# RMSNorm with tanh-GELU on one core: six rows per partition instead of four, in units of three, with one last store and one gamma transfer

## The chip, the cores and the metric

One core of one Trainium2 chip. The time is the device time of one execution in microseconds (us). "Before" and "after" name the two kernels. A statement such as "317.44 us" is a median of single executions; a ratio is the mean time of one kernel's fast runs over the mean of the other kernel's fast runs of the same rounds, so it is not quite the ratio of the medians quoted beside it. An interval is 95%. A run is called slow when it is over 1.5% above the fastest of the same kernel.

## The reference

```python
# x: 8 x 1024 x 2048 float32, gamma: 2048, eps = 1e-5
rms = np.sqrt(np.mean(x ** 2, axis=-1, keepdims=True) + eps)
out = gamma * x / rms
return 0.5 * out * (1 + np.tanh(np.sqrt(2 / np.pi) * (out + 0.044715 * out ** 3)))
```

There are 8192 rows of 8 KB: 67.1 MB in, 67.1 MB out, and little arithmetic per byte.

## The kernel before

A group is 128 partitions times four rows. Row r of partition p lies beside row r+1 of the same partition in HBM, so one partition's share of a group is one contiguous piece of 32 KB. Six buffers on chip hold six groups. ACT (ScalarE) squares and sums each row, GpSimd makes 1/rms from the sum, VectorE multiplies by gamma (which TensorE has spread over the partitions into PSUM), ACT applies the GELU with 1/rms as its scale, and the store goes out from ACT's queue. Loads go out from SyncE's queue.

```python
ROWS = 4
SLOTS = 6
...
store_pieces = {
    0: [(R, [(0, NARROW), (NARROW, R * D)])],            # a narrow first store of 512 B per partition
    G - 1: [(1, [(r * D, r * D + D)]) for r in range(R)], # last group: a store per row
}
...
def load(g):
    nc.sync.dma_start(out=slot[g % SLOTS], in_=x3[g])
...
for g in range(G + 1):
    if g < G:
        squares(g)
        inverse_rms(g)
        scale(g)
    if g:
        gelu_store(g - 1)                  # one group behind
        if g - 1 + SLOTS < G:
            load(g - 1 + SLOTS)            # waits for that store to land
```

Of the kernel before, what the change touches and what calls it, by code (L numbers as in the profile page):

```python
# [1 line left out]

# [4 lines left out]

FP32 = mybir.dt.float32
ALU = mybir.AluOpType
ACT = mybir.ActivationFunctionType  # L10

P = 128
ROWS = 4
SLOTS = 6

GW = 32
CHUNK = 512

NARROW = 128


@with_exitstack
def kernel(
    ctx: ExitStack,
    tc: tile.TileContext,
    x: bass.AP,
    gamma: bass.AP,
    eps: bass.AP,
    out: bass.AP,
):  # L30




    nc = tc.nc
    D = x.shape[-1]
    R = ROWS
    eps_f = float(eps)
    x3 = x.rearrange("b s d -> (b s) d").rearrange("(g p r) d -> g p r d", p=P, r=R)
    o3 = out.rearrange("b s d -> (b s) d").rearrange("(g p r) d -> g p r d", p=P, r=R)  # L40
    G = x3.shape[0]

    sbuf = ctx.enter_context(tc.tile_pool(name="sbuf", bufs=1))
    psum = ctx.enter_context(
        tc.tile_pool(name="psum", bufs=1, space=bass.MemoryType.PSUM)
    )
    slot = [sbuf.tile([P, R, D], FP32, name=f"slot{i}") for i in range(SLOTS)]
    gamma_row = sbuf.tile([1, D // GW, GW + 4], FP32, name="gamma_row")
    ones = sbuf.tile([1, P], FP32, name="ones")
    warm = sbuf.tile([1, 1], FP32, name="warm")  # L50
    power = sbuf.tile([P, R], FP32, name="power")
    ssq = sbuf.tile([P, G, R], FP32, name="ssq")
    rstd = sbuf.tile([P, G, R], FP32, name="rstd")
    ms = sbuf.tile([P, R], FP32, name="ms")
    y = sbuf.tile([P, R], FP32, name="y")
    z = sbuf.tile([P, R], FP32, name="z")
    gamma_ps = psum.tile([P, D], FP32, name="gamma_ps")
    junk = psum.tile([P, D], FP32, name="junk")


    whole = [(R, [(0, R * D)])]
    store_pieces = {
        0: [(R, [(0, NARROW), (NARROW, R * D)])],
        G - 1: [(1, [(r * D, r * D + D)]) for r in range(R)],
    }
    scale_pieces = {G - 1: [(0, 1), (1, 1), (2, 1), (3, 1)]}

    def load(g):
        nc.sync.dma_start(out=slot[g % SLOTS], in_=x3[g])  # L69

    def squares(g):
        for r in range(R):
            nc.scalar.activation(  # L73
                out=junk,
                in_=slot[g % SLOTS][:, r, :],
                func=ACT.Square,
                accum_out=ssq[:, g, r : r + 1],
            )

    def scale(g):  # L80
        for r, n in scale_pieces.get(g, [(0, R)]):
            rows = slot[g % SLOTS][:, r : r + n, :]
            nc.vector.tensor_tensor(  # L83
                out=rows,
                in0=rows,
                in1=gamma_ps.unsqueeze(1).to_broadcast([P, n, D]),
                op=ALU.mult,
            )

    def inverse_rms(g):  # L90

        v = nc.gpsimd
        v.tensor_scalar(  # L93
            out=ms, in0=ssq[:, g, :], scalar1=1.0 / D, scalar2=eps_f,
            op0=ALU.mult, op1=ALU.add,
        )
        v.tensor_tensor(out=y, in0=ms, in1=power, op=ALU.pow)  # L97
        v.tensor_tensor(out=z, in0=y, in1=y, op=ALU.mult)  # L98
        v.tensor_tensor(out=z, in0=z, in1=ms, op=ALU.mult)  # L99
        v.tensor_scalar(  # L100
            out=z, in0=z, scalar1=-0.5, scalar2=1.5, op0=ALU.mult, op1=ALU.add
        )
        v.tensor_tensor(out=rstd[:, g, :], in0=z, in1=y, op=ALU.mult)  # L103

    def gelu_store(g):
        flat = slot[g % SLOTS].rearrange("p r d -> p (r d)")
        dst = o3[g].rearrange("p r d -> p (r d)")
        row = 0
        for n, stores in store_pieces.get(g, whole):
            for r in range(row, row + n):  # L110
                nc.scalar.activation(  # L111
                    out=slot[g % SLOTS][:, r, :],
                    in_=slot[g % SLOTS][:, r, :],
                    func=ACT.Gelu_apprx_tanh,
                    scale=rstd[:, g, r : r + 1],
                )
            row += n
            for a, b in stores:
                nc.scalar.dma_start(out=dst[:, a:b], in_=flat[:, a:b])  # L119

    with tc.manual_schedule():
        for k in range(0, D, CHUNK):
            nc.scalar.dma_start(
                out=gamma_row[:, k // GW : (k + CHUNK) // GW, 0:GW],
                in_=gamma[k : k + CHUNK].rearrange("(o a b) -> o a b", o=1, b=GW),
            )
        for g in range(SLOTS):
            load(g)
        nc.gpsimd.memset(power, -0.5)  # L129
        nc.vector.memset(warm, 0.0)  # L130
        nc.vector.memset(ones, 1.0)  # L131
        nc.scalar.activation(out=warm, in_=warm, func=ACT.Gelu_apprx_tanh)  # L132
        for k in range(0, D, CHUNK):
            nc.tensor.matmul(  # L134
                out=gamma_ps[:, k : k + CHUNK],
                lhsT=ones,
                rhs=gamma_row[:, k // GW : (k + CHUNK) // GW, 0:GW],
                start=True,
                stop=True,
            )  # L140
        for g in range(G + 1):
            if g < G:
                squares(g)
                inverse_rms(g)
                scale(g)
            if g:
                gelu_store(g - 1)
                if g - 1 + SLOTS < G:
                    load(g - 1 + SLOTS)


# [1 line left out]
_INS = ['x', 'gamma', 'eps']  # L153
_OUTS = [((8, 1024, 2048), 'float32')]

_NUMBERS = {'eps': 9.999999747378752e-06}


# [26 lines left out]
```

## Time and profile before

| | before |
|---|---|
| time, median of the first 3 runs | 317.41 us (317.26 to 317.46) |
| span of the profiled run | 315.5 us |
| ACT / VectorE busy | 80% / 44% |
| DMA queues, share of the 16 engines' span | 49.7% + 49.4% |
| HBM traffic | 425 GB/s over the span |

The page is read from the share of busy time to the slices to the DMA queues. The prediction shows the lines and reads them.

One thing goes beyond the page. The trace holds a record of each DMA packet (queue, start, duration, bytes). No view prints it; where a number below comes from it, I say "packet record".

### The profile page before, as it was taken

The numbers are of one execution on the slowest core, as the hardware profiler recorded it, in microseconds if no ns is written. First come the engines' busy times: TensorE is split into PE (matmuls) and PEld (weight loads), VectorE is DVE, ScalarE is ACT, GpSimd is POOL, SyncE is SP. The second block draws the span as 40 slices with busy tenths as digits, with TensorE's granted clock in tenths as the row PEclk, the third lists the DMA queues.
The fourth block names the chain that finished last, engine by engine and source line by source line (L and its number), as shares of the span: only waits on it lengthen the run. The fifth ranks groups of instructions, "written<-read, shape, count | busy, mean of one in ns | idle before, by whom it ended". The sixth has DMA issues, their size and how long they took to land.

```text
span 315.5 us, 479 instructions
## 1 busy us (share of the span) xinstructions
PE 7.9 (3%) x8; PEld 2.1 (1%) x8; DVE 139.4 (44%) x21; ACT 251.2 (80%) x194; POOL 32.3 (10%) x101
## 2 busy tenths in 40 slices
PE   0810000000000000000000000000000000000000
PEld 0200000000000000000000000000000000000000
DVE  0028909091918282827328082370824609480000
ACT  1289999999999999989596895969959599598500
POOL 0020202020202020202020020200202002020000
DMA  8999999999999999999999999999999999999997
GB/s 329 404 461 403 459 413 396 453 406 462 403 461 407 457 407 458 411 453 416 449 428 440 432 432 432 432 440 424 446 416 453 411 453 411 453 415 449 416 418 314
DMA packets 5315, 134.25 MB, mean 426 GB/s; under 512 B 704, under 2 KB 832, under 8 KB 832
## 3 DMA queue, kind: packets, MB, share of 16 engines
q1 hardware_dynamic: 2304, 67.11, 49.7%
q10 hardware_dynamic: 3008, 67.12, 49.4%
q14 instruction: 3, 0.02, 0.0%
HBM read 67.12 MB, written 67.11 MB: 425 GB/s over the span
## 4 chain that ended last, share of the span: by engine, by line
ACT 38%; DMA 32%; another core or an unknown queue 18%; issue 5%; ACTq 1%; SPq 0%
ACT slot L111 21%; DMA slot<-in_x_dram 16%; ACT junk L73 16%; DMA out_dram<-slot 15%; ACTq L119 1%; SPq L69 0%; ACTq L111 0%; ACTq L73 0%
## 5 line engine op out<-in xcount | busy, mean ns | idle before, releaser
L83 DVE TENSOR_TENSOR slot<-slot,gamma_ps 128x8192 f32<-128x8192 f32 (+1 forms) x19 | 139.2, 7338 | 142.3 <-ACT junk L73 142.3
L73 ACT ACTIVATE junk<-slot 128x2048 f32<-128x2048 f32 x64 | 120.4, 1881 | 40.8 <-DMA slot<-in_x_dram 36.8
L111 ACT ACTIVATE slot<-slot,rstd 128x2048 f32<-128x2048 f32 x64 | 123.0, 1987 | 1.7 <-ACT slot L111 1.7
L93 POOL TENSOR_SCALAR ms<-ssq 128x4 f32<-128x4 f32 x16 | 3.1, 194 | 242.8 <-ACT junk L73 242.8
L97 POOL TENSOR_TENSOR y<-ms,power 128x4 f32<-128x4 f32 x16 | 16.1, 1009 | 1.3
L73 ACT ACTIVATION_READ_ACCUMULATOR junk<-slot 128x1 f32 x64 | 11.9, 186 | 0.0
L134 PE MATMUL gamma_ps<-gamma_row,ones 1*128 1x512 f32 x8 | 7.9, 1112 | 9.2 <-DMA gamma_row<-in_gamma_dram 9.2
L132 ACT ACT_TABLE_LOAD x1 | 1.3, 1283 | 3.3 <-issue 3.3
L99 POOL TENSOR_TENSOR z<-z,ms 128x4 f32<-128x4 f32 x16 | 3.2, 201 | 1.3
L103 POOL TENSOR_TENSOR rstd<-z,y 128x4 f32<-128x4 f32 x16 | 3.2, 200 | 1.3
L98 POOL TENSOR_TENSOR z<-y 128x4 f32<-128x4 f32 x16 | 3.2, 200 | 1.3
L100 POOL TENSOR_SCALAR z<-z 128x4 f32<-128x4 f32 x16 | 3.1, 195 | 1.4
L134 PEld LDWEIGHTS gamma_ps<-gamma_row,ones 1*128 1x128 f32 x8 | 2.1, 306 | 13.4 <-issue 8.7
L130 DVE MEMSET warm<- 1x1 f32 x1 | 0.1, 59 | 0.8 <-PEq L166 0.8
L132 ACT ACTIVATE warm<-warm 1x1 f32<-1x1 f32 x1 | 0.2, 203 | 0.0
L131 DVE MEMSET ones<- 1x128 f32 x1 | 0.2, 165 | 0.0
L129 POOL MEMSET power<- 128x4 f32 x1 | 0.1, 102 | 0.3 <-POOLq L166 0.3
L166 POOL MEMSET const-float32-0.0<- 128x1 f32 x1 | 0.1, 99 | 0.2 <-issue 0.2
L166 POOL MEMSET const-bfloat16-1.0<- 128x1 bf16 x1 | 0.1, 102 | 0.0
L166 POOL MEMSET const-uint8-127<- 128x1 uint8 x1 | 0.1, 102 | 0.0
L166 POOL MEMSET const-float32-1.0<- 128x1 f32 x1 | 0.1, 99 | 0.0
## 6 DMA issues: line engine op xcount, KB each, us to landing
slot<-in_x_dram SPq DMA_DIRECT2D x16, 4096.0 KB, 29.9
out_dram<-slot ACTq DMA_DIRECT2D x14, 4096.0 KB, 43.3
out_dram<-slot ACTq DMA_DIRECT2D x4, 1024.0 KB, 17.5
out_dram<-slot ACTq DMA_DIRECT2D x1, 4032.0 KB, 28.5
gamma_row<-in_gamma_dram ACTq DMA_DIRECT2D x4, 2.0 KB, 10.3
out_dram<-slot ACTq DMA_DIRECT2D x1, 64.0 KB, 14.4
```

The lines of the kernel that those rows point to most:

```text
L73: nc.scalar.activation(out=junk, in_=slot[g % SLOTS][:, r, :], func=ACT.Square, accum_out=ssq[:, g, r : r + 1],)
L83: nc.vector.tensor_tensor(out=rows, in0=rows, in1=gamma_ps.unsqueeze(1).to_broadcast([P, n, D]), op=ALU.mult,)
L93: v.tensor_scalar(out=ms, in0=ssq[:, g, :], scalar1=1.0 / D, scalar2=eps_f, op0=ALU.mult, op1=ALU.add,)
L97: v.tensor_tensor(out=y, in0=ms, in1=power, op=ALU.pow)
L98: v.tensor_tensor(out=z, in0=y, in1=y, op=ALU.mult)
L99: v.tensor_tensor(out=z, in0=z, in1=ms, op=ALU.mult)
L100: v.tensor_scalar(out=z, in0=z, scalar1=-0.5, scalar2=1.5, op0=ALU.mult, op1=ALU.add)
L103: v.tensor_tensor(out=rstd[:, g, :], in0=z, in1=y, op=ALU.mult)
L111: nc.scalar.activation(out=slot[g % SLOTS][:, r, :], in_=slot[g % SLOTS][:, r, :], func=ACT.Gelu_apprx_tanh, scale=rstd[:, g, r : r + 1],)
L119: nc.scalar.dma_start(out=dst[:, a:b], in_=flat[:, a:b])
L132: nc.scalar.activation(out=warm, in_=warm, func=ACT.Gelu_apprx_tanh)
L134: nc.tensor.matmul(out=gamma_ps[:, k : k + CHUNK], lhsT=ones, rhs=gamma_row[:, k // GW : (k + CHUNK) // GW, 0:GW], start=True, stop=True,)
```

## The change

The intent: larger and fewer packets (48 KB instead of 32 KB per partition), fewer transfers, a shorter tail of stores, a gamma transfer that needs one piece per DMA engine. To fit, the six buffers become four. Since a group is now longer, its compute is cut into two units of three rows, so that VectorE can begin while ACT still squares. The diff is abridged.

```diff
-ROWS = 4
-SLOTS = 6
+ROWS = 6
+UNIT = 3
+SLOTS = 4
-GW = 32
-CHUNK = 512
+GW = 128
...
+    rows = [ROWS] * (N // ROWS) + ([N % ROWS] if N % ROWS else [])   # ten groups of 6, one of 4
...
-        G - 1: [(1, [(r * D, r * D + D)]) for r in range(R)],
...
-        for k in range(0, D, CHUNK):
-            nc.scalar.dma_start(out=gamma_row[...], in_=gamma[k : k + CHUNK]...)
+        nc.scalar.dma_start(out=gamma_row[:, :, 0:GW], in_=gamma.rearrange(...))
...
-        for g in range(G + 1):
-            if g < G:
-                squares(g); inverse_rms(g); scale(g)
-            if g:
-                gelu_store(g - 1)
+        for g in range(G - 1):
+            for r in range(0, ROWS, UNIT):
+                norm(g, r, UNIT, UNIT)       # squares, 1/rms, gamma
+            for r in range(0, ROWS, UNIT):
+                gelu(g, r, UNIT)
+            store(g, ...)                    # group 0: narrow, then the rest
+            if g + SLOTS < G:
+                load(g + SLOTS, 0, rows[g + SLOTS])
+        norm(G - 1, 0, rows[G - 1], 1); gelu(...); store(...)
```

More of the change, by code (lines that the diff above doesn't have):

```diff
@@ L36, with part @@
     D = x.shape[-1]
-    R = ROWS
     eps_f = float(eps)
-    x3 = x.rearrange("b s d -> (b s) d").rearrange("(g p r) d -> g p r d", p=P, r=R)
-    o3 = out.rearrange("b s d -> (b s) d").rearrange("(g p r) d -> g p r d", p=P, r=R)
-    G = x3.shape[0]
+    x2 = x.rearrange("b s d -> (b s) d")
+    o2 = out.rearrange("b s d -> (b s) d")
+    N = x2.shape[0] // P
+    rows = [ROWS] * (N // ROWS) + ([N % ROWS] if N % ROWS else [])
+    G = len(rows)
+    def part(a, g):
+        first = g * ROWS * P
+        return a[first : first + rows[g] * P].rearrange("(p r) d -> p r d", p=P)
     sbuf = ctx.enter_context(tc.tile_pool(name="sbuf", bufs=1))
@@ L46 @@
     )
-    slot = [sbuf.tile([P, R, D], FP32, name=f"slot{i}") for i in range(SLOTS)]
-    gamma_row = sbuf.tile([1, D // GW, GW + 4], FP32, name="gamma_row")
+    slot = [sbuf.tile([P, ROWS, D], FP32, name=f"slot{i}") for i in range(SLOTS)]
+    gamma_row = sbuf.tile([1, D // GW, GW + 16], FP32, name="gamma_row")
     ones = sbuf.tile([1, P], FP32, name="ones")
     warm = sbuf.tile([1, 1], FP32, name="warm")
-    power = sbuf.tile([P, R], FP32, name="power")
-    ssq = sbuf.tile([P, G, R], FP32, name="ssq")
@@ L53 @@
-    rstd = sbuf.tile([P, G, R], FP32, name="rstd")
-    ms = sbuf.tile([P, R], FP32, name="ms")
-    y = sbuf.tile([P, R], FP32, name="y")
-    z = sbuf.tile([P, R], FP32, name="z")
+    power = sbuf.tile([P, ROWS], FP32, name="power")
+    ssq = sbuf.tile([P, G, ROWS], FP32, name="ssq")
+    rstd = sbuf.tile([P, G, ROWS], FP32, name="rstd")
+    ms = sbuf.tile([P, ROWS], FP32, name="ms")
+    y = sbuf.tile([P, ROWS], FP32, name="y")
+    z = sbuf.tile([P, ROWS], FP32, name="z")
     gamma_ps = psum.tile([P, D], FP32, name="gamma_ps")
@@ L58, with load @@
     junk = psum.tile([P, D], FP32, name="junk")
-    whole = [(R, [(0, R * D)])]
-    store_pieces = {
-        0: [(R, [(0, NARROW), (NARROW, R * D)])],
-        G - 1: [(1, [(r * D, r * D + D)]) for r in range(R)],
-    }
-    scale_pieces = {G - 1: [(0, 1), (1, 1), (2, 1), (3, 1)]}
-    def load(g):
-        nc.sync.dma_start(out=slot[g % SLOTS], in_=x3[g])
-    def squares(g):
-        for r in range(R):
+    def load(g, r, n):
+        nc.sync.dma_start(
+            out=slot[g % SLOTS][:, r : r + n, :], in_=part(x2, g)[:, r : r + n, :]
+        )
@@ L73, in squares, with norm @@
+    def norm(g, r, n, step):
+        for q in range(r, r + n):
             nc.scalar.activation(
                 out=junk,
-                in_=slot[g % SLOTS][:, r, :],
+                in_=slot[g % SLOTS][:, q, :],
                 func=ACT.Square,
-                accum_out=ssq[:, g, r : r + 1],
+                accum_out=ssq[:, g, q : q + 1],
             )
-    def scale(g):
-        for r, n in scale_pieces.get(g, [(0, R)]):
-            rows = slot[g % SLOTS][:, r : r + n, :]
+        v = nc.gpsimd
+        m_, y_, z_ = ms[:, 0:n], y[:, 0:n], z[:, 0:n]
+        v.tensor_scalar(
+            out=m_, in0=ssq[:, g, r : r + n], scalar1=1.0 / D, scalar2=eps_f,
+            op0=ALU.mult, op1=ALU.add,
+        )
+        v.tensor_tensor(out=y_, in0=m_, in1=power[:, 0:n], op=ALU.pow)
+        v.tensor_tensor(out=z_, in0=y_, in1=y_, op=ALU.mult)
+        v.tensor_tensor(out=z_, in0=z_, in1=m_, op=ALU.mult)
+        v.tensor_scalar(
+            out=z_, in0=z_, scalar1=-0.5, scalar2=1.5, op0=ALU.mult, op1=ALU.add
+        )
+        v.tensor_tensor(out=rstd[:, g, r : r + n], in0=z_, in1=y_, op=ALU.mult)
+        for q in range(r, r + n, step):
+            data = slot[g % SLOTS][:, q : q + step, :]
@@ L83, in scale @@
             nc.vector.tensor_tensor(
-                out=rows,
-                in0=rows,
-                in1=gamma_ps.unsqueeze(1).to_broadcast([P, n, D]),
+                out=data,
+                in0=data,
+                in1=gamma_ps.unsqueeze(1).to_broadcast([P, step, D]),
                 op=ALU.mult,
             )
-    def inverse_rms(g):
-        v = nc.gpsimd
-        v.tensor_scalar(
-            out=ms, in0=ssq[:, g, :], scalar1=1.0 / D, scalar2=eps_f,
-            op0=ALU.mult, op1=ALU.add,
-        )
-        v.tensor_tensor(out=y, in0=ms, in1=power, op=ALU.pow)
-        v.tensor_tensor(out=z, in0=y, in1=y, op=ALU.mult)
-        v.tensor_tensor(out=z, in0=z, in1=ms, op=ALU.mult)
-        v.tensor_scalar(
-            out=z, in0=z, scalar1=-0.5, scalar2=1.5, op0=ALU.mult, op1=ALU.add
-        )
-        v.tensor_tensor(out=rstd[:, g, :], in0=z, in1=y, op=ALU.mult)
@@ L105, in gelu_store @@
-    def gelu_store(g):
-        flat = slot[g % SLOTS].rearrange("p r d -> p (r d)")
-        dst = o3[g].rearrange("p r d -> p (r d)")
-        row = 0
-        for n, stores in store_pieces.get(g, whole):
-            for r in range(row, row + n):
-                nc.scalar.activation(
-                    out=slot[g % SLOTS][:, r, :],
-                    in_=slot[g % SLOTS][:, r, :],
-                    func=ACT.Gelu_apprx_tanh,
-                    scale=rstd[:, g, r : r + 1],
-                )
-            row += n
-            for a, b in stores:
-                nc.scalar.dma_start(out=dst[:, a:b], in_=flat[:, a:b])
@@ L121, with gelu @@
-    with tc.manual_schedule():
-        for k in range(0, D, CHUNK):
-            nc.scalar.dma_start(
-                out=gamma_row[:, k // GW : (k + CHUNK) // GW, 0:GW],
-                in_=gamma[k : k + CHUNK].rearrange("(o a b) -> o a b", o=1, b=GW),
-            )
+    def gelu(g, r, n):
+        for q in range(r, r + n):
+            row = slot[g % SLOTS][:, q, :]
+            nc.scalar.activation(
+                out=row, in_=row, func=ACT.Gelu_apprx_tanh,
+                scale=rstd[:, g, q : q + 1],
+            )
@@ L127, with store @@
+    def store(g, a, b):
+        flat = slot[g % SLOTS].rearrange("p r d -> p (r d)")
+        dst = part(o2, g).rearrange("p r d -> p (r d)")
+        nc.scalar.dma_start(out=dst[:, a:b], in_=flat[:, a:b])
+    with tc.manual_schedule():
+        nc.scalar.dma_start(
+            out=gamma_row[:, :, 0:GW],
+            in_=gamma.rearrange("(o a b) -> o a b", o=1, b=GW),
+        )
         for g in range(SLOTS):
-            load(g)
+            load(g, 0, rows[g])
         nc.gpsimd.memset(power, -0.5)
@@ L132 @@
         nc.scalar.activation(out=warm, in_=warm, func=ACT.Gelu_apprx_tanh)
-        for k in range(0, D, CHUNK):
+        for k in range(0, D, 512):
             nc.tensor.matmul(
-                out=gamma_ps[:, k : k + CHUNK],
+                out=gamma_ps[:, k : k + 512],
                 lhsT=ones,
-                rhs=gamma_row[:, k // GW : (k + CHUNK) // GW, 0:GW],
+                rhs=gamma_row[:, k // GW : (k + 512) // GW, 0:GW],
                 start=True,
@@ L140 @@
             )
-        for g in range(G + 1):
-            if g < G:
-                squares(g)
-                inverse_rms(g)
-                scale(g)
-            if g:
-                gelu_store(g - 1)
-                if g - 1 + SLOTS < G:
-                    load(g - 1 + SLOTS)
+        for g in range(G - 1):
[3 more added lines that the diff above has]
+                gelu(g, r, UNIT)
+            if g == 0:
+                store(g, 0, NARROW)
+                store(g, NARROW, ROWS * D)
+            else:
+                store(g, 0, ROWS * D)
+            if g + SLOTS < G:
+                load(g + SLOTS, 0, rows[g + SLOTS])
+        g = G - 1
+        norm(g, 0, rows[g], 1)
+        gelu(g, 0, rows[g])
+        store(g, 0, rows[g] * D)
 _INS = ['x', 'gamma', 'eps']
```

## The prediction

> **What bounds the kernel now.** I read the page from the top: busy shares, the slices, the DMA queues; then the stretches in time, the waits, the end of the chain of waits, and last the trace's record of every DMA packet (start, duration, size), which no view prints and from which I quote medians and sums.
>
> ```profile
> span 315.5 us, 479 instructions
> PE 7.9 (3%) x8; PEld 2.1 (1%) x8; DVE 139.4 (44%) x21; ACT 251.2 (80%) x194; POOL 32.3 (10%) x101
> ...
> DMA  8999999999999999999999999999999999999997
> ...
> DMA packets 5315, 134.25 MB, mean 426 GB/s; under 512 B 704, under 2 KB 832, under 8 KB 832
> ...
> q1 hardware_dynamic: 2304, 67.11, 49.7%
> q10 hardware_dynamic: 3008, 67.12, 49.4%
> ```
>
> The busiest compute engine, ACT, is at 80%; the two DMA queues (q1 loads, q10 stores and gamma) together hold the 16 DMA engines for 99.1% of the span. The slices are full from the second to the last but one. The stretches in time say the same with rates (DMA share and GB/s are the last two columns):
>
> ```profile
> 0.00:1.70 1.70, 0.00 (x0) 0.00 (x0) 0.22 (x2) 0.00 (x0) 0.29 (x5) 1.00 0.00 0
> ...
> 60.00:120.00 60.00, 0.00 (x0) 0.00 (x0) 34.42 (x4) 58.02 (x45) 8.00 (x24) 1.00 1.01 436
> ...
> 297.40:313.00 15.60, 0.00 (x0) 0.00 (x0) 0.00 (x0) 0.00 (x0) 0.00 (x0) 1.00 1.00 425
> 313.00:315.50 2.50, 0.00 (x0) 0.00 (x0) 0.00 (x0) 0.00 (x0) 0.00 (x0) 1.00 0.17 72
> ```
>
> After 297.4 us no engine computes and the DMA is still full for 15.6 us: the last stores wait behind earlier ones, not on arithmetic. The waits agree: ACT waits on data, and SyncE waits on stores before it may reuse a buffer.
>
> ```profile
> ACT junk L73 <- DMA slot<-in_x_dram: 36.8, 10, 8.7
> ...
> SPq L69 <- DMA out_dram<-slot: 224.3, 10, 53.7
> ```
>
> The chain of waits ends on ACT at 297 us with "ACT slot L111" and gives 38% to ACT. I don't take that as the bound: it follows semaphores, and here the queue behind the last issue decides. The packet record runs from 1.73 to 314.30 us, and its busy time over 16 engines is 312.66 us: as much as that stretch is long. So the time is 1.73 us of start, some 312.6 us of uninterrupted DMA, 1.16 us from the last packet to the end of the span, and 1.9 us outside the span (317.41 less 315.5).
>
> **What a packet costs.** A load or store of a group is one packet per partition, 8 per DMA engine: 32768 B takes 1.213 us (median of 2048 loads), 8192 B 0.309 us (the last four stores). Slope: 0.904 us over 24576 B, 36.78 us per MB, or 27.19 GB/s per engine, 435 GB/s for 16. Fixed part: 0.309 - 0.301 = 0.0077 us. It gives 1.194 us for the 32256 B packets of the first store; the record has 1.194. Per engine before:
> - payload 8.3886 MB at 36.784: 308.57 us
> - data packets: loads 16 x 8 = 128; stores 15 x 8 + 8 narrow + 4 x 8 small = 160; 288 x 0.0077 = 2.22 us
> - completion packets of 4 B: 640 / 16 = 40 x 0.009 = 0.36 us; gamma 4 x 0.013 = 0.05 us
> - packets longer than their kind's median: 1.47 us, of which 0.72 at the very first loads (about 2.0 us instead of 1.213) and 0.68 between 45 and 48 us, when the first large store begins.
> The sum, 312.67, closes on the 312.66 measured. This is the account that I change.
>
> **What the Trainium skill says.**
> - "Perfetto Trace Analysis", Roofline: a single active core may draw more than its 358 GB/s share of HBM but is bounded by its 16 DMA engines, about 435 GB/s together. The trace agrees: 436 GB/s in the stretch above.
> - "DMA: Bandwidth & Descriptors", Why small descriptors are slow: a fixed cost of about 3 cycles per packet inside the DMA engine. The trace agrees that there is one, and that it is tiny; the two sizes put it at 0.0077 us, which I use.
> - The same page, Specifications: line rate wants pieces of at least 512 B. That is the intent for gamma, but by the record a 128 B packet took 0.013 us and a 512 B one 0.027 us, and gamma has four of the former per engine in all: there is next to nothing to win.
> - The same page, Queues, rings and completion order: each engine takes turns between its queues packet by packet. The trace agrees: the narrow first store's eight 512 B packets per engine lie one by one between 32 KB loads, from 36.5 to 45.7 us.
>
> **The change, part by part.**
> - Groups of six rows: per engine, loads are 10 x 8 + 8 = 88 packets and stores 88 + 8 narrow = 96. That is 184 for 288: 104 x 0.0077 = 0.80 us saved, all of it on the path since the engines never idle. Of these, 24 come from one last store in place of four.
> - Fewer transfers: 11 loads, 12 stores and one gamma, so 24 completion packets instead of 40: 16 x 0.009 = 0.14 us saved.
> - Gamma: one 512 B packet per engine (0.027) for four of 0.013: 0.02 us saved. It lands later if it sits behind several 48 KB loads, but the first multiplication needs it only at about 24 us.
> - Payload unchanged: 308.57 us. New sum 308.57 + 1.42 + 0.22 + 0.03 + 1.47 = 311.71, against 312.67: 0.96 us less.
> - Compute: the same 64 squares and 64 gelus. A unit of three rows costs VectorE, from 8.687 us at 8192 elements and 2.280 us at 2048, 2.280 + 4096 x 1.043 ns = 6.55 us. GpSimd runs its six small operations 21 times instead of 16. None of it is on the path while stores are queued.
>
> **Does the DMA stay fed?** The interleaving of one group's gelus with the next one's squares goes: each group now does its six squares, then its six gelus. ACT per group: first multiplication after three squares (3 x 2.035 = 6.1 us), done at 12.7; the second done at 19.3; its three gelus (1.9 us each) end near 25.1; with the store issue 25.5 us. Two 6.29 MB transfers take 8 x 2 x 1.816 = 29 us of DMA. So ACT is faster than the DMA by 3.5 us a group. Hand schedule, in us: load 0 lands at 1.7 + 0.7 + 14.5, a little over 17, ACT begins near 18.2; store 0 is issued at 43.3, store 1 at 68.8, store 2 at 94.3. The narrow pieces now each wait for a 48 KB load, 8 x 1.84 = 14.7 us, so the bulk of store 0 begins near 57 and lands near 76, sharing with the rest of load 3 until about 64. Store 1 is by then queued for 7 us. Store 1 ends near 103 (store 2 queued since 94), each later store 29 us on; load g+4 starts as store g lands. ACT becomes bound by the loads at about group 8. At the end: load 10 lands near 269, its four rows are done near 294, and stores 8 and 9 occupy the DMA until about 301. The margins are 7 us at both ends, so I expect no hole.
>
> **The rivals.**
> - Starvation: four buffers for six. For it: the same 24 rows on chip are handed over in bigger pieces, and ACT has bubbles of 0.5 us in each unit. Against: the 7 us margins and 15.6 us of stores left at the end of before. If it came, some 3 to 8 us once, 320 to 325.
> - Restarts of the load queue. In before, two or three loads are always queued (longest issue to landing 64.7 us); now load 3 is finished 12 us before load 4 can start, and later each load is ready only 2 or 3 us before the one ahead ends. If a queue that restarts beside the other one stalls everything as at 45 to 48 us (0.68 us), one event gives 317.1 and six give 320. Against: the switch from mixed traffic to stores alone, at 271 us, cost nothing in the record.
> - A real gain from larger pieces or the shorter tail. Against: the rate is per engine and already met; the tail's arithmetic is hidden under 15.6 us of stores. The floor is 1.73 + 308.57 + 1.16 + 1.9 = 313.4, 1.3% below the present time, so over 2% faster is out of reach.
>
> **Range and chances.** 317.41 - 0.96 = 316.45; a tenth for the chance of a restart makes 316.5. The engines end unevenly now (0.7 us of mean idle after 310 us), and this may shift by 0.4 us either way; the low end is 315.7. The high end, 317.6, allows one or two restarts. Within 2% 0.96; slower 0.03, which takes 6.3 us of lost DMA time; faster 0.01.
>
> **What would show it.** DMA packets near 3,350 (per engine 184 + 24 + 1, times 16); 48 KB packets at 1.816 us; the two queues still over 98% together; the slices 9 throughout; ACT near 80%, VectorE near 45%. Wrong: a slice of 8 or less around 60 to 80 us or near the end (starvation), or 48 KB packets longer than 1.82 us by the sum of the queue shares (restarts), or packets split to 32 KB or less, which would take away the 0.8 us.

## The result, and the profile after

After: 317.72 us, median of four runs (317.39 to 318.61), beside 317.44 us for before; ratio 1.0014, interval 0.9993 to 1.0035. That is the same within noise, and 0.12 us above the upper end of the predicted range. Two more series of the unchanged kernel (below) gave medians of 317.90 and 318.66 us. All 16 runs of after have a median of 318.04 us and lie between 317.12 and 319.49; the 48 runs of before in all sessions have 317.44 and lie between 317.14 and 318.01. So the expected gain of 1 us didn't come, and a scatter came that before did not have.

The profiled run of after took 317.39 us, the quickest of its four. Its page:

```profile
span 315.6 us, 497 instructions
...
PE 7.2 (2%) x8; PEld 2.5 (1%) x8; DVE 139.3 (44%) x26; ACT 253.0 (80%) x194; POOL 38.9 (12%) x131
...
DMA  8999999999999999999999999999999999999996
...
DMA packets 3347, 134.25 MB, mean 425 GB/s; under 512 B 384, under 2 KB 528, under 8 KB 528
...
q1 hardware_dynamic: 1584, 67.11, 49.7%
q10 hardware_dynamic: 1760, 67.12, 49.2%
```

There are 3347 packets for 5315, the predicted number (3350). The compute shares are the predicted ones. The queues hold 98.9% instead of 99.1%. No slice is under 8 but the last, and that one is a 6 where before had a 7.

The timeline of ACT's queue after (start, duration, queue, operation): the narrow store, then the stores of groups 0 to 3:

```profile
37.70 0.36 ACTq L116 DMA_DIRECT2D out_dram<-slot  x1
...
43.43 0.34 ACTq L116 DMA_DIRECT2D out_dram<-slot  x1
...
68.84 0.34 ACTq L116 DMA_DIRECT2D out_dram<-slot  x1
...
94.26 0.34 ACTq L116 DMA_DIRECT2D out_dram<-slot  x1
...
119.67 0.34 ACTq L116 DMA_DIRECT2D out_dram<-slot  x1
```

The hand schedule had 43.3, 68.8 and 94.3. The waits after (who waited for what, us in total, times, longest), first the engines', then SyncE's queue:

```profile
ACT junk L75 <- DMA slot<-in_x_dram: 25.0, 4, 15.6
...
ACT slot L107 <- DVE slot L97: 9.1, 14, 0.7
```

```profile
SPq L68 <- DMA out_dram<-slot: 242.5, 8, 53.3
```

ACT's waits for VectorE inside a group, at most 0.7 us each, are the bubbles that the prediction allowed for; none reaches the DMA.

The last stretches in time after (the last two columns are DMA share and GB/s):

```profile
297.40:313.00 15.60, 0.00 (x0) 0.00 (x0) 0.00 (x0) 1.69 (x1) 0.00 (x0) 1.00 0.97 421
313.00:315.60 2.60, 0.00 (x0) 0.00 (x0) 0.00 (x0) 0.00 (x0) 0.00 (x0) 1.00 0.03 13
```

Before had a share of 1.00 up to 313.0 us and 0.17 after it; after has 0.97 and 0.03. These figures have to be read with care. Recomputed from the packet record, they come out when each packet is counted wholly in the stretch in which it begins; with packets cut at 313.0 us, the shares are 1.01 and 0.23 in before and 1.00 and 0.12 in after. So 13 GB/s means that about one packet of 32 KB began in the last 2.6 us; it does not tell how many engines were still at work. The ends of the engines tell that. From the packet record, the times at which the sixteen engines ended (each engine's last completion packet):

```
before  313.27 313.33 313.36 313.38 313.38 313.39 313.39 313.47 313.48 313.51 313.54 313.56 313.74 313.84 313.98 314.30
after   312.83 312.94 312.96 313.01 313.10 313.14 313.18 313.20 313.25 313.31 313.38 313.42 313.46 313.57 313.58 314.44
```

The mean end moved from 313.56 to 313.30 us, the last engine from 314.30 to 314.44. The kernel waits for the last one. From now on I split each profiled run so: span = mean end + (last engine less mean) + tail.

### The profile page after: what moved, and what is told of

It is laid out like the page before. It is cut to its first block, busy times and chain, and to the rows that moved or that the text cites. A ratio compares the mean times of both kernels' runs of the same rounds, so it can differ in the third digit from the quotient of the medians.

```text
span 315.6 us, 497 instructions
## 1 busy us (share of the span) xinstructions
PE 7.2 (2%) x8; PEld 2.5 (1%) x8; DVE 139.3 (44%) x26; ACT 253.0 (80%) x194; POOL 38.9 (12%) x131
## 2 busy tenths in 40 slices
DMA packets 3347, 134.25 MB, mean 425 GB/s; under 512 B 384, under 2 KB 528, under 8 KB 528
## 4 chain that ended last, share of the span: by engine, by line
DMA 32%; ACT 29%; DVE 22%; issue 9%; ACTq 1%; POOL 1%; POOLq 0%; DVEq 0%; SPq 0%
DVE slot L97 22%; DMA slot<-in_x_dram 17%; ACT junk L75 15%; DMA out_dram<-slot 15%; ACT slot L107 14%; ACTq L116 1%; POOL y L88 0%; POOLq L183 0%; POOL z L90 0%; POOL z L89 0%; POOL ms L84 0%; POOL z L91 0%; ACTq L107 0%; DVEq L97 0%; SPq L68 0%
## 5 line engine op out<-in xcount | busy, mean ns | idle before, releaser
L97 DVE TENSOR_TENSOR slot<-slot,gamma_ps 128x6144 f32<-128x6144 f32 (+1 forms) x24 | 139.1, 5839 | 151.6 <-ACT junk L75 151.6
L84 POOL TENSOR_SCALAR ms<-ssq 128x3 f32<-128x3 f32 (+1 forms) x21 | 4.2, 198 | 243.3 <-ACT junk L75 243.3
L88 POOL TENSOR_TENSOR y<-ms,power 128x3 f32<-128x3 f32 (+1 forms) x21 | 18.0, 859 | 1.7
L130 PE MATMUL gamma_ps<-gamma_row,ones 1*128 1x512 f32 x8 | 7.2, 1072 | 9.5 <-DMA gamma_row<-in_gamma_dram 9.5
L91 POOL TENSOR_SCALAR z<-z 128x3 f32<-128x3 f32 (+1 forms) x21 | 4.2, 198 | 1.8
L94 POOL TENSOR_TENSOR rstd<-z,y 128x3 f32<-128x3 f32 (+1 forms) x21 | 4.1, 196 | 1.8
L90 POOL TENSOR_TENSOR z<-z,ms 128x3 f32<-128x3 f32 (+1 forms) x21 | 4.1, 194 | 1.6
L89 POOL TENSOR_TENSOR z<-y 128x3 f32<-128x3 f32 (+1 forms) x21 | 4.1, 193 | 1.6
```

Source lines behind the costliest of these rows:

```text
L84: v.tensor_scalar(out=m_, in0=ssq[:, g, r : r + n], scalar1=1.0 / D, scalar2=eps_f, op0=ALU.mult, op1=ALU.add,)
L88: v.tensor_tensor(out=y_, in0=m_, in1=power[:, 0:n], op=ALU.pow)
L89: v.tensor_tensor(out=z_, in0=y_, in1=y_, op=ALU.mult)
L90: v.tensor_tensor(out=z_, in0=z_, in1=m_, op=ALU.mult)
L91: v.tensor_scalar(out=z_, in0=z_, scalar1=-0.5, scalar2=1.5, op0=ALU.mult, op1=ALU.add)
L94: v.tensor_tensor(out=rstd[:, g, r : r + n], in0=z_, in1=y_, op=ALU.mult)
```

## The experiments

Theory G, "given back": the packet saving is there on the mean, but it is given back by larger one-time stalls (the first loads; the first large store beside loads) and by one engine that ends late. Rivals: H, holes in the DMA in the slower runs; S, 48 KB packets cost more all the time; B, the tight four buffers; and, against all of these, the order of computing or the extra GpSimd instructions.

"Stretch" below, where it is said of packets, is their time over the median of their size, summed and divided by 16 engines; from the packet record. ("Stretches in time" are the windows of a view.) The first stall counts packets that begin before 8 us, the second those from 8 to 100 us.

### The changed kernel again

No edit.

> The changed kernel again, unchanged, for a second profile and a closer ratio. Theory G (given back): the saving per packet is there, but the two one-time stalls grew with the packet (first loads, first large store: 1.40 us before, 1.79 us after) and the engines end less evenly. Then: mean busy time of an engine 311.8 to 312.3 us, one-time stalls 1.6 to 2.0 us, end of the packet record 0.6 us or more after the mean end of the engines, times scattered over 317.3 to 318.7, ratio 1.000 to 1.003. Rival H (holes): in the slower runs the DMA runs dry somewhere; then a profile of a slower run shows a slice of 8 or less or idle engines in the middle. Rival S (steady cost): 48 KB packets cost more in the steady state in some runs; then their sum less the median is above 0.3 us outside the two stalls.

Measured: 317.90 us (317.12 to 319.31, 6 runs), ratio 1.0018 (0.9999 to 1.0036). The profiled run took 317.80 us: mean end 313.39, last engine 1.47 us later, stalls 0.75 and 1.02 us. The mean busy time of an engine is 312.00 us, as in the first profile of after. The slices are all 9 from the second to the last but one. Rival H falls for this run, and so does S: past 100 us all packets together are only 0.11 us per engine over their median.

### The changed kernel a third time

No edit; it ran beside the runs with pieces below.

> The changed kernel a third time, beside the runs with smaller packets, so that its scatter is known on the same chip. As before: times over more than 1 us, median 317.6 to 318.0, mean end of the engines 313.3 to 313.4 us, last engine 1.0 us or more after it.

Measured: 318.66 us (317.78 to 319.49, 6 runs), ratio 1.0039 (1.0024 to 1.0054). The profiled run, 319.23 us, is one of the longest, and shows what makes it long. Stretches in time:

```profile
297.40:313.00 15.60, 0.00 (x0) 0.00 (x0) 0.00 (x0) 3.07 (x2) 0.00 (x0) 1.00 0.98 422
313.00:317.50 4.50, 0.00 (x0) 0.00 (x0) 0.00 (x0) 0.00 (x0) 0.00 (x0) 1.00 0.04 15
```

Up to 313 us the shares agree with those of the first profile; then this run goes on for 4.5 us instead of 2.6. (The 0.04 again counts packets where they begin; cut at 313.0 us it is 0.1, or 1.7 engines of sixteen on the mean.) The ends from the packet record: fourteen engines between 312.88 and 313.55 us, one at 314.07, the last at 316.29. The mean end is 313.45, 0.15 us off the first profile; the last engine is 2.84 us after the mean instead of 1.14. Span 317.45 = 313.45 + 2.84 + 1.16.

The completion packets (4 B, one per engine and transfer) show how the lateness builds up. By how much the last engine is later than the fifteenth is 0.03 us when load 0 lands, 1.12 us at load 3 (the first stores run beside it), 0.95 at load 4, then 1.59, 1.73 and 2.16 us at loads 5, 6 and 7. It grows round by round, by single load packets: one that starts at 111.94 us takes 2.46 us instead of 1.82, one at 170.73 takes 2.25; each begins exactly one packet (1.81 us) after the last engine's completion of the load before it (110.13 and 168.92), which is how I know them for that engine's.

### Everything but the size: the changed code at four rows

```diff
-ROWS = 6
-UNIT = 3
-SLOTS = 4
+ROWS = 4
+UNIT = 2
+SLOTS = 6
...
```

> The changed kernel's code (units, one last store, one gamma transfer, squares and gelus of a group not interleaved with the next) with groups of four rows in six buffers, so the packets and buffers of the kernel before. If the scatter and the late last engine come from the 48 KB packets or the four buffers: mean end of the engines 313.4 to 313.6 us as before, last engine less than 0.9 us after the mean, times 317.2 to 317.9 with the scatter of before, ratio 0.999 to 1.000. If they come from the order of the computing or from the 30 extra GpSimd instructions (instruction fetches on the same DMA engines): scatter over 1 us and ratio 1.001 to 1.003 here too.

Measured: 317.47 us (317.23 to 317.56, 5 runs), ratio 1.000 (0.9988 to 1.0012). Profile of a run of 317.56: mean end 313.59, last engine 0.83 us later. The new order of computing, the single gamma transfer, the single last store and even more GpSimd instructions (191; 131 in after, 101 in before) are in this kernel, and the scatter is not. So the scatter comes with the six rows in four buffers, unless it is the chip: this series ran on chip 8, where the unchanged after was not run; its two later series ran on chips 9 and 3.

### The last store alone

The kernel before, with one store for its last group:

```diff
-        G - 1: [(1, [(r * D, r * D + D)]) for r in range(R)],
```

> The kernel before with its last group stored by one transfer instead of four, nothing else: 24 packets (0.18 us) and 3 completion packets (0.03 us) less per engine. The account: 317.2, ratio 0.9993. The tail's arithmetic is hidden under 15 us of stores; if that is wrong and the last store is late by the three gelus, 319 to 323.

Measured: 317.34 us (317.18 to 317.89, 5 runs), ratio 0.9992 (0.9979 to 1.0005). This agrees with the 0.2 us expected and cannot be told from nothing. Beside the changed code at four rows it is the only version that lies at or below before, and I call it the same. The profiled run (317.89, the slowest of the five) had a mean end of 313.54 and a last engine 1.21 us after it: late engines occur at 32 KB too, but up to 1.2 us in what I saw, not 2.8.

### Same transfers, smaller packets

The decisive pair. Each partition's six rows are taken from two (or three) places in HBM, so that one transfer of the same bytes into the same buffer is made of pieces of 24 KB (or 16 KB). Transfers, buffers, waits and instructions stay, but that group 0's bulk is stored by two transfers, and that the last group of four rows stays in one piece of 32 KB in the run with three.

```diff
+PIECES = 2        # and 3 in the second run
...
-        return a[first : ...].rearrange("(p r) d -> p r d", p=P)
+        n = PIECES if rows[g] % PIECES == 0 else 1
+        return a[first : ...].rearrange("(h p r) d -> p h (r d)", h=n, p=P)
...
```

> The changed kernel with each partition's six rows taken from two places, so that the same transfers, buffers, waits and instructions move 24 KB packets instead of 48 KB ones (the first group's bulk is stored by two transfers). Account: some 176 packets per engine more at 0.004 to 0.007, 0.7 to 1.2 us on the mean end. Theory P (the scatter and the late last engine come from the 48 KB packets): stall at the first stores 0.4 to 0.6 us, last engine 0.6 to 0.9 us after the mean, scatter under 0.5 us, time 317.5 to 318.0. Theory B (they come from four buffers and a load queue that nearly runs dry): scatter over 1 us stays, last engine 1.2 us or more after the mean, time 318.3 to 319.

> The same with three pieces of two rows, 16 KB packets. Account: 1.5 to 2.3 us on the mean end against the changed kernel. Theory P: stall at the first stores 0.3 to 0.4 us, scatter under 0.4 us, 318.2 to 319.2. Theory B: as the changed kernel plus the account, 319 to 320.5 with scatter over 1 us.

Measured, with 24 KB: 317.77 us (317.58 to 318.08, 5 runs), ratio 1.0012 (1.0000 to 1.0024). With 16 KB: 318.71 us (318.51 to 319.00, 5 runs), ratio 1.0040 (1.0028 to 1.0052). Beside them on the same chip, 48 KB packets gave 317.78 to 319.49. The packet counts show that the edit did what it should; DMA packets of the 24 KB run, then of the 16 KB run:

```profile
DMA packets 6179, 134.25 MB, mean 424 GB/s; under 512 B 400, under 2 KB 544, under 8 KB 544
```

```profile
DMA packets 8483, 134.25 MB, mean 424 GB/s; under 512 B 400, under 2 KB 544, under 8 KB 544
```

The mean ends are 313.77 and 314.80 us: more packets cost time on the mean, 0.3 to 0.5 us for 176 and 1.35 to 1.5 us for 320 more per engine, against the three profiles at 48 KB. For 176 that is under the 0.7 expected; for 320 at or just under the low end, 1.5. The scatter is 0.5 us in both and 1.7 us at 48 KB. So theory P of the expectation, the packet size, holds for the scatter, and theory B, the four buffers, falls. One rival is left by these two runs alone: the edit also changes which rows in HBM a partition's pieces come from. The run at four rows, where a partition's piece is contiguous as in after, is as quiet, which speaks against it. Two details missed: the last engine was 1.27 us after the mean in the profile at 24 KB (a run of 318.08, the slowest of five; expected at most 0.9), and the second stall at 16 KB was 1.15 us (expected 0.3 to 0.4). The stall at the first stores does not simply grow with the packet.

### Two rows at both ends

Ten groups of six between a first and a last group of two, to make the first packets small:

```diff
-    rows = [ROWS] * (N // ROWS) + ([N % ROWS] if N % ROWS else [])
+    rows = [2] + [ROWS] * 10 + [2]
...
```

> The changed kernel with the first and the last group of two rows (16 KB packets) and ten groups of six between. The account: 200 data packets per engine for 184 (+0.12 us) and two transfers more (+0.02). Theory G: the first-load stall falls from 0.89 to about 0.55 us and the first-store stall from 0.90 to about 0.5 (straight line through 32 and 48 KB), so 0.6 us less on the mean, and less scatter: 316.6 to 317.2, ratio to before 0.998 to 0.999. If the stalls belong to the first 48 KB packets rather than to the first packets, they stay at 0.9 and the time is 317.6 or more. Rival H: with two rows in the first slot the loads run out before the first store lands: a hole near 30 to 60 us, 319 or more.

Measured: four fast runs of 318.17 to 321.79 us (median 319.88), and two slow ones of 323.28 and 324.99 us; ratio of the fast ones 1.0075 (1.004 to 1.0111). A miss. In the profile (318.81, one of the quicker ones) the first stall is 0.83 us, not smaller; the stretch about the first small store is only 0.1 us, but when the loads restart at 61 us beside the first 48 KB stores, packets take up to 3.2 us instead of 1.8, some two for each engine, 1.1 us per engine in all. So in this run the second stall came at the first meeting of large loads and large stores, and moved with it. There is no hole: busy engines, slow packets.

### Groups of two rows throughout

The kernel before with two rows in twelve buffers:

```diff
-ROWS = 4
-SLOTS = 6
+ROWS = 2
+SLOTS = 12
-    scale_pieces = {G - 1: [(0, 1), (1, 1), (2, 1), (3, 1)]}
+    scale_pieces = {G - 1: [(0, 1), (1, 1)]}
```

> The kernel before with groups of two rows in twelve buffers (16 KB packets), a test of the account in the other direction. Packets: 528 per engine for 288 (+1.85 us at 0.0077) and 70 completion packets for 40 (+0.27). Theory G: plus 2.1 us on the account, minus 0.17 and 0.22 us of smaller stalls: 319.1, 318.7 to 319.6, with less scatter than 0.3 us. If packets had no fixed cost: 317.0. If a store has to wait on a shared semaphore or ACT, with 0.9 us a group to spare, becomes the bound: 320 and more, with holes.

Measured: 332.56 us (332.01 to 332.74, 4 runs), ratio 1.047. The rival of holes came, from a source that is not the change's. Its slices, the wait of ACT, and the wait of SyncE:

```profile
DMA  7999999999999999999999999999999999866668
```

```profile
ACT junk L73 <- DMA slot<-in_x_dram: 55.5, 8, 15.1
```

```profile
SPq L69 <- DMA slot<-in_x_dram: 51.5, 9, 19.2
```

SyncE holds back loads until other loads have landed: with so many short transfers the built program reuses a completion semaphore while an earlier transfer still holds it. ACT misses 15 us of data at 230 to 245 us, falls behind, and the DMA runs dry from 290 us on. The full stretch of this run still tests the account. Once the loads and stores are in step, a round of one load and one store took (spacing of the landings of loads, packet record) 9.73 us here, 19.37 us in before and 29.00 us in after. That is a straight line: 9.63 us for every 16 KB of packet size, and about 0.1 us for the sixteen packets and two completions whatever their size. So the fixed cost is real, but some 0.005 us per packet, not 0.0077, since in the record an engine begins a packet 3 to 7 ns before the one ahead ends. And once the stalls are past, 48 KB packets are not slow: S falls again. This run also shows ends that are even to 0.14 us, presumably because after a hole the engines start level.

### Stores in halves

```diff
-                store(g, NARROW, ROWS * D)
+                store(g, NARROW, UNIT * D)
             else:
-                store(g, 0, ROWS * D)
+                store(g, 0, UNIT * D)
+            store(g, UNIT * D, ROWS * D)
...
```

> The changed kernel with each store as two transfers of three rows (24 KB packets), loads left at 48 KB. Turns go packet by packet, so loads move twice as fast as stores while both run; each load then ends some 7 us before the next can start, and the load queue restarts six times beside running stores. Account: 88 packets more, +0.4 us, 12 completions +0.1. If restarts cost (the run with two-row edges had 1.0 us at one): 0.3 to 1 us each, time 319 to 323 and wide scatter, with packets over their median at every restart. If that one stall was only the first large store beside a large load: one stall of 0.5 to 0.9 us in all, 317.7 to 318.3.

Measured: 318.56 us (318.16 to 318.77, 5 runs), ratio 1.0033 (1.0021 to 1.0045). Mean end 314.09 us, last engine 0.87 us after it, stretch of 0.73 and 1.03 us, and 0.36 past 100 us. It lies between the two expectations: restarts of the load queue cost something, but below 0.1 us each, and the scatter is small although loads are still 48 KB. The restarts that I had made the second rival are not what takes the microsecond.

### A ramp of small first stores

Group 0 in six stores of one row after the narrow one:

```diff
-                store(g, NARROW, ROWS * D)
+                store(g, NARROW, D)
+                for r in range(1, ROWS):
+                    store(g, r * D, r * D + D)
```

> The changed kernel with the first group stored in six transfers of one row (8 KB packets) after the narrow one. If the stall belongs to the first store beside loads and grows with its packet (0.35 us at 16 KB, 0.7 to 0.8 at 32 KB, 0.9 to 1.0 at 48 KB): 0.2 us there, none later, 317.0 to 317.4. If it belongs to the first 48 KB store beside 48 KB loads, it moves to the restart of the loads near 80 us and stays 0.9 us or more: 317.8 to 320, as with the two-row edges.

Measured: 319.50 us (317.74 to 320.25, 6 runs), ratio 1.0052 (1.0032 to 1.0071). The second expectation, not the first. In the profile (320.25) the second stall is 0.99 us, but the stretched packets go on: 77 of them (by more than 0.02 us) past 100 us, against 4 in before and 7 in after. Mean end 314.38, last engine 2.75 us after it.

### Without the narrow first store, after and before

```diff
# after                                            # before
-            if g == 0:                            -        0: [(R, [(0, NARROW), (NARROW, R * D)])],
-                store(g, 0, NARROW)
-                store(g, NARROW, ROWS * D)
-            else:
-                store(g, 0, ROWS * D)
+            store(g, 0, ROWS * D)
```

> The changed kernel without the narrow first store: the first group goes out as one 48 KB-packet transfer as soon as it is ready, near 45 us, with 15 us of loads still queued, and lands some 10 us sooner. If the narrow pieces do no more than delay it: the same stall of 0.9 us, at 46 to 49 us, time as the changed kernel, 317.4 to 318.2. If they soften the first store: a larger stall, 1.3 us or more, and 318.2 or more.

> The kernel before without its narrow first store. The changed kernel lost 6 us by this. If that loss comes with the size of the packets that first meet: some 1 to 3 us here (318.5 to 320.5), packets over their median near 40 us. If it has nothing to do with the size: 6 us here too, 323.

Measured, after without it: 323.60 us (322.63 to 325.19, 4 runs), ratio 1.0200 (1.0176 to 1.0224). Before without it: 317.51 us (317.31 to 318.24, 4 runs), ratio 1.0009 (0.9995 to 1.0024). At 48 KB the narrow store is worth 5.6 us against the median of after (318.04), at 32 KB next to nothing, less than I expected. Three stretches of after, with the narrow store and then without it:

```profile
46.00:60.00 14.00, 0.00 (x0) 0.00 (x0) 10.08 (x2) 13.29 (x12) 3.66 (x12) 1.00 1.01 406
60.00:80.00 20.00, 0.00 (x0) 0.00 (x0) 7.61 (x2) 18.75 (x16) 1.83 (x6) 1.00 1.03 444
80.00:100.00 20.00, 0.00 (x0) 0.00 (x0) 8.35 (x2) 18.27 (x13) 1.83 (x6) 1.00 1.01 435
```

```profile
46.00:60.00 14.00, 0.00 (x0) 0.00 (x0) 9.76 (x2) 13.26 (x14) 3.66 (x12) 1.00 1.05 393
60.00:80.00 20.00, 0.00 (x0) 0.00 (x0) 7.61 (x2) 18.75 (x16) 1.83 (x6) 1.00 0.99 378
80.00:100.00 20.00, 0.00 (x0) 0.00 (x0) 8.68 (x2) 18.27 (x13) 1.83 (x6) 1.00 0.98 396
```

Read the last two columns together. The DMA share is near 1 in both, so no engine is idle, but the rate falls to 378 GB/s: the packets are long, 5.69 us per engine of stretch between 8 and 100 us. A share of busy time alone would not have shown it. With 32 KB packets the same edit left 0.81 us of stretch there (0.71 with the narrow store). So how large packets of the two queues first meet matters at 48 KB, and hardly at 32 KB.

### Small packets at the start only, or after it only

To tell whether the late engine is made at the start or later: 24 KB pieces in the first four groups alone, or in all but those. The diff is against the run with two pieces.

```diff
-        n = PIECES if rows[g] % PIECES == 0 else 1
+        n = PIECES if g < SLOTS else 1       # second run: g >= SLOTS
```

> 24 KB packets in the first four groups, 48 KB in the others. Account: 65 packets per engine more than the changed kernel, +0.3 to 0.4 us on the mean end (313.7). If the late engine is made at the start: scatter under 0.6 us, last engine under 1.1 us after the mean, median 317.3 to 317.7. If it is made in the steady state by 48 KB packets: scatter over 1 us stays, median 318.0 to 318.8.

> 48 KB packets in the first four groups, 24 KB in the others. Account: 112 packets per engine more, +0.5 to 0.7 us on the mean end (313.9 to 314.1). If the late engine is made at the start and only carried along: scatter over 1 us stays, median 318.3 to 319. If it is made in the steady state: scatter under 0.6 us, median 317.7 to 318.1.

Measured: 320.72 us (320.32 to 323.14, 6 runs), ratio 1.0115 (1.009 to 1.014); and 325.77 us (325.45 to 326.58, the four fast runs of 5), ratio 1.0266 (1.0253 to 1.0279). Both are misses, far outside both expectations. In the first, 130 packets past 100 us are stretched, 33.3 us in sum over the engines, against 0.9 us in the first profile of after. In the second the profile fell in the slow state (its run took 333.57 us), so I take no time from it; its record shows one engine falling behind from load to load, by 17.3 us at the last one, and the DMA then running dry. Both edits cost more than the thing to be measured. It is tempting to blame packets of different sizes in the two queues, but that is not shown: the stores in halves had 24 KB beside 48 KB all along, and took 318.56 us. The cause, and the question that these two runs were made for, stay open.

## Why the prediction was right or wrong, point by point

The splits of the profiled runs, in us:

| run (time) | mean end | last engine less mean | tail | span |
|---|---|---|---|---|
| before (317.24) | 313.56 | 0.74 | 1.16 | 315.46 |
| after (317.39) | 313.30 | 1.14 | 1.16 | 315.60 |
| after again (317.80) | 313.39 | 1.47 | 1.16 | 316.02 |
| after, third (319.23) | 313.45 | 2.84 | 1.16 | 317.45 |
| changed code, four rows (317.56) | 313.59 | 0.83 | 1.36 | 315.77 |
| after, 24 KB pieces (318.08) | 313.77 | 1.27 | 1.26 | 316.30 |
| after, 16 KB pieces (318.71) | 314.80 | 0.87 | 1.25 | 316.92 |

**What bounds the kernel: right.** The DMA is full in every profile of after (the third shows one slice of 8 near 60 us, but its packets too sum to the whole time up to the mean end, 312.10 us for 311.74). The bound on any gain stands too: no version came near 2% faster.

**The packet count and the size of the packets: right.** 3347 packets, 48 KB at 1.815 us (1.816 predicted), none split.

**"Does the DMA stay fed?": right.** The stores were issued within 0.2 us of the hand schedule up to group 2, and there is no hole. The tail margin was tighter than said: the last group's gelus end at 299.1 us, not 294, with the store ahead of it landing at 303.1 to 304.8. Starvation did not come.

**Restarts as a rival: right to doubt them, for this kernel.** In after the load queue restarts near 80 us, and packets between 60 and 100 us are 0.02 us per engine over their median.

**"104 x 0.0077 = 0.80 us saved, all of it on the path": the term was too large.** The 0.0077 us is the fixed part of a packet's duration, but consecutive packets of an engine overlap, so the sum of durations counts some of it twice. In before the sum, 312.66 us, is 0.83 us longer than the stretch from the first packet to the mean end; in after 0.43 us. So 0.4 us of the 0.96 saved in the sum was never on the path. The close match of 312.66 with the stretch to the last packet was luck: an overlap of 0.83 us stood against 0.74 us in which the mean engine had already ended.

**"1.47 us of stalls", carried over unchanged: wrong.** The stretch of packets is 1.89 us in after (1.89 and 1.98 in the other two profiles), 0.4 us more. I took the first loads and the first large store to cost the same whatever the packet. They are 0.71 and 0.71 us in before, 0.88 and 0.92 in after. The size of the growth is rough: in two other profiles with 32 KB packets (the last store alone, the changed code at four rows) the stretch is 1.58 and 1.63 us, which leaves 0.3 us.

Together these two leave 0.1 to 0.2 us of the 0.96. Measured, the mean end of after lies 0.26, 0.17 and 0.11 us before that of before.

**"The engines end unevenly ..., and this may shift by 0.4 us either way": the step that failed.** It moved one way, by 0.40, 0.73 and 2.10 us. In the first profile it more than cancels the rest: -0.26 + 0.40 = +0.14 us of span, as measured. In the third it is the whole of the difference: -0.11 + 2.10 = +1.99 us. I had worked the account for the mean engine and given the last one a symmetric margin, with the mean idle time after 310 us as its only ground. The kernel ends with its slowest engine, and a sum over sixteen engines cannot show that one. Predicted were -0.96 us and the profiles have +0.14 and +1.99: of the 1.10 us between them in the first, 0.70 are in the two terms above and 0.40 here; of the 2.95 in the third, 0.85 and 2.10.

The packet record also shows something that I had overlooked. The kernel's instructions are fetched by the same DMA engines, 8 KB at a time: three times while it runs, in before and in after alike (five times in the changed code at four rows). In the first profile of after one fetch begins at 245.14 us; with the longer packet behind it it takes 0.65 us of one engine. The last engine's lateness after the mean is 0.35 us at load 8, before the fetch, and 0.83 at load 9, after it; one load packet at 272.99 us, 0.34 us longer than its kind, brings it to 1.15. So more than half of this lateness is where a fetch happened to fall, and says nothing about packet size. The same goes for 32 KB: the last engine at four rows and the one with the last store alone, followed back packet by packet (each begins a few ns before the one ahead of it on its engine ends), had each taken two fetches, 1.1 and 1.0 us with the packets behind them. But the last engines of the second and third profile of after took none. There the load packets themselves were stretched, past 100 us by 0.8 us in the second and in the third by 0.65 and 0.43 us in the two packets above alone. This is the part that goes with 48 KB.

What is shown: the scatter comes with the 48 KB packets, since with the same transfers, buffers and code at 24 or 16 KB, on the same chip, it is 0.5 us for 1.7, and with the same code at 32 KB it is 0.3 us. With 48 KB in the loads alone (stores in halves) it is 0.6 us. In the profile of a long run the excess is one late engine; that all the scatter is that, is inferred from three profiles. What is not shown: why one engine, why its load packets are stretched again round after round, and whether this is set at the first meeting of loads and stores. That it follows the first meeting is only suggested: the engine is 1.12 us late at load 3 in the third profile, and every run in which large packets met otherwise (two-row edges, ramp, no narrow store) scatters by 2.5 us or more in its fast runs. Nothing here shows what happens in the memory.

## What to carry to other kernels

When the DMA is the bound, make the account for the mean engine, then ask separately what the last engine does: look at the last stretch of the profile, and at the spread of repeated times, before counting on a gain of a few tenths of a per cent. Here the fixed cost at 32 KB was only some 0.5% of a packet's duration (0.005 to 0.0077 of 1.213 us); 48 KB won nothing measurable any more, and cost evenness. Read DMA share and GB/s side by side: in the run without the narrow store a share of 0.99 came with 378 GB/s instead of 444, which meant slow packets. And before reading a short stretch at the end, ask whether the view cuts packets at its border.

## What the Trainium skill lacked or had wrong

- "DMA: Bandwidth & Descriptors", Rules for kernel authors: it asks for at least 1 MiB per transfer and for coalescing, and gives there no upper limit for the contiguous piece of one partition. Here, on one chip, 48 KB pieces gave 317.78 to 319.49 us, the same transfers in 24 KB pieces 317.58 to 318.08.
- The same page, Why small descriptors are slow: it gives a fixed cost of about 3 cycles per packet, and no time for it. Here the durations have 0.0077 us per packet, and rounds of 16 packets some 0.005 (9.73, 19.37 and 29.00 us at 16, 32 and 48 KB), so part of it overlaps other packets.
- The same page, Queues, rings and completion order: it tells of turns packet by packet, but not that the first meeting of large loads and large stores stretches packets (0.7 to 0.9 us per engine at 32 KB, 0.9 to 1.1 at 48 KB, 5.69 us at 48 KB without a narrow first store).
- The same page, Latency and other measured facts: it names two engines as usually slower, with a best guess that holds only for transfers that GpSimd issues. Here none is issued by GpSimd, all engines have equal bytes, and one still ended up to 2.84 us after the mean (the record does not name it).
- No page says what an instruction fetch costs a full DMA: in after three fetches of 8 KB after the start, 0.31 us each, with the data packet behind it 0.09 to 0.34 us longer.
